# Low parts of the feed-forward input weights made by a negated copy on ScalarE and an adding DMA

## The chip, the cores and the metric

The kernel runs on one core of one Trainium2 chip. The metric is the device time of one execution in microseconds (us); the time before is the median of three runs. The core has five engines that each work through their own instructions in order: TensorE (PE in the profile, with its weight loads as PEld), VectorE (DVE), ScalarE (ACT), GpSimd (POOL) and SyncE (SP, which here only issues DMAs). Engines wait for each other, and for DMAs, by semaphores.

## The reference

The reference is a trunk of two layers on 512 tokens of width 1024 in float32: a gated linear attention (GLA) mixer with its feed-forward part, then a gated DeltaNet (GDN) mixer with its feed-forward part, each followed by a residual and a LayerNorm. What the change touches is the feed-forward part, which both layers have:

```python
def conv_ffn(x, w_in, conv_w, w_out):
    h = causal_dwconv(x @ w_in, conv_w)          # w_in: 1024 x 5632, conv_w: 3 x 5632
    gate, up = jnp.split(h, 2, axis=-1)          # 2816 columns each
    return (jax.nn.gelu(gate, approximate=False) * up) @ w_out
```

## The kernel before

Every large product is done in three matmuls on a reduced float32 format (float32r): each operand is split into a high part, its value rounded to float32r, and a low part, the difference. The products high x high, high x low and low x high are summed in PSUM. For a weight tile the split is two instructions in `split_out` (line 698): ScalarE copies the raw tile to `wh` with rounding (CAST), and VectorE subtracts it from the raw tile into `wl` (TENSOR_TENSOR).

The feed-forward input product runs over items. One item is 128 columns of `w_in`: the raw weights (128 partitions x 1024 float32, 512 KB) are loaded by a DMA on SP's queue (line 304), split, and used in 24 matmuls of 128x512 (8 blocks of the contraction, three products each, the third of which reads `wl`). Items alternate between a gate block and an up block. After an item ScalarE scales the PSUM bank by the last tap of the convolution (line 991), VectorE adds the two other taps (line 993), and for a gate block ScalarE applies Gelu (line 1011); an up block is multiplied by its gate.

The 44 items of one layer come in three groups of 16, 16 and 12. After each of the first two groups the matching rows of the output weights are multiplied in the folded form (`folded`, PSUM tiles `fold`, 14 weight items of 12 matmuls): sums of quarters of `w_out`, with tiles `b` and `raw` loaded by line 390. The last group is followed by the plain product with the last rows of `w_out` (`out_rows`, PSUM tiles `tm`): its weights are six more `raw` loads (line 321), and each half is split into a slot of its own (in the profile these slots are called `fh`, `fl` or `b`, because they are cut from tiles that the group before has left). The first rows of `tm` need the activations of all six row blocks of the last group, the last item's too.

Buffers set how far ahead this runs. There are three `raw` tiles, shared by the input weights, the `raw` quarters of the fold and the output weights, and four pairs of `wh` and `wl`. A new load into a raw tile waits until its last reader is done; a split waits until the item four before has been used. SP issues loads in one order, and a load that waits holds those behind it. The program is written as one sequence (`prefetch` issues an item's load and split two items ahead, three in the fold, five near the end of the last group), and a scheduler then sets each engine's order from its estimates; only PE's order is mostly pinned.

GpSimd does the affine step of the residual at the start of each feed-forward part (lines 903 and 904) and issues a few DMAs.

Of the kernel before, what the change touches and what calls it, by code (L numbers as in the profile page):

```python
# [8 lines left out]
F32 = mybir.dt.float32  # L9
# [4 lines left out]
ALU = mybir.AluOpType  # L14

P = 128
D = 1024
S = 512
NTB = S // P
NC = D // P  # L20
DFF = 2816
# [46 lines left out]
def blk(i, n=P):  # L68
    return slice(i * n, i * n + n)


class Trunk:
# [214 lines left out]
    def issue(self, item):  # L287

        nc = self.nc
        if item[0] == "rep":  # L290
            return self.issue_rep(*item[1:])
        if item[0] == "pad":
            return self.issue_pad(*item[1:])
        if item[0] == "fold":
            return self.issue_fold(*item[1:])
        if item[0] == "gated":
            return self.issue_gated(*item[1:])
        raw = self.rp.tile([P, 1024], F32, name=self.uid("raw"), tag="raw")
        used = 1024
        if item[0] == "fm":  # L300
            _, w, col = item
            r3 = raw.rearrange("p (c f) -> p c f", c=NC)
            w3 = w[:, col:col + P].rearrange("(c p) f -> p c f", p=P)
            part = lambda queue, c, n: queue.dma_start(r3[:, c:c + n, :], w3[:, c:c + n, :])
            if self.issued > 1:
                part(nc.sync, 0, NC)
            else:
                if self.issued == 0:
                    part(nc.scalar, 0, 4)
                    self.arriving(0, 1)  # L310
                else:
                    part(nc.sync, 0, 4)
                    self.arriving(1, 1)
                self.late.append(lambda: part(nc.sync, 4, 4))
                if self.issued:
                    for load in self.late:
                        load()
        else:
            _, w, row, n, col, _ = item
            used = n * S  # L320
            self.load = nc.sync.dma_start(
                raw[:, :used].rearrange("p (j f) -> p j f", j=n),
                w[row:row + n * P, col:col + S].rearrange("(j p) f -> p j f", p=P))
        if self.in_slots(item):
            w = []
            for j in range(used // S):
                wh, wl = self.room("wsh"), self.room("wsl")
                self.slotted = self.split_out(wh, wl, raw[:, blk(j, S)])
                self.vec(0.7)
                w.append((wh, wl))  # L330
            return w
        self.held += 1
        wh = self.wp.tile([P, 1024], F32R, name=self.uid("wh"), tag="wh")
        wl = self.wp.tile([P, 1024], F32R, name=self.uid("wl"), tag="wl")
        pieces = [blk(j, S) for j in range(used // S)] if self.issued < 2 else [slice(0, used)]
        split = lambda cols: self.split_out(wh[:, cols], wl[:, cols], raw[:, cols])
        if self.issued < 2:
            self.pieces += [lambda cols=cols: split(cols) for cols in pieces]
        elif self.issued < 4:
            self.opening(*split(pieces[0]))  # L340
        else:
            self.split = parts = split(pieces[0])
            for ins, other in zip(parts, self.after):
                if other is not None:
                    self.behind(ins, other)
        self.vec(1.24)
        return [(wh[:, blk(j, S)], wl[:, blk(j, S)]) for j in range(used // S)]
# [348 lines left out]

    def split_out(self, dst_h, dst_l, src):
        return self.nc.scalar.copy(dst_h, src), self.nc.vector.tensor_sub(dst_l, src, dst_h)  # L698

    def opening(self, *parts):  # L700

        if self.first is not None:
            for ins, other in zip(parts, self.first):
                self.behind(ins, other)
        self.first = parts
# [1321 lines left out]
```

## Time and profile before

| what | value |
| --- | --- |
| median of three runs | 1227.69 us (1227.67 to 1228.21) |
| profiled execution, span from first to last instruction | 1226.6 us (the page has no other time of this execution) |
| PE busy | 1219.4 us, 99% of the span |
| DVE busy | 928.2 us, 76% |
| ACT busy | 604.0 us, 49% |
| POOL busy | 115.1 us, 9% |
| DMA, mean over the span | 109 GB/s |
| feed-forward input product and folds, first layer | 222 to 535 us |
| the same, second layer | 873 to 1186 us |
| granted TensorE clock | 1.000 |

Times in the trace are counted from the first instruction. A row of the timeline reads: start, duration, engine, line, operation, output tile <- input tiles, shape, count, and in brackets the idle time of the engine just before with what ended it. Rows of DMA issues read: output <- input, issuing queue, count, size of one, and median time from issue to landing.

### The profile page before, as it was taken

Reading aid. Unit: us, or ns where it says so; the run is one execution under the profiler, and the core shown is the slowest. Engines: PE = TensorE matmul, PEld = TensorE weight load, DVE = VectorE, ACT = ScalarE, POOL = GpSimd, SP = SyncE. Lnnn points to the kernel's source line nnn. Section 1 sums busy time; section 2 is a strip of 40 time slices with the busy share of each in tenths; the row PEclk is TensorE's granted clock in tenths of the full one; section 3 lists DMA queues with packets and bytes.
Section 4 is the critical chain, followed back from the end, with each engine's and each line's share of the span. In section 5 each row is a group of like instructions: output and inputs, shape, how many; then the busy total and the mean of one; then the engine's idle time right before and its main releaser. Section 6 shows DMA issues by size and latency. Waiting matters only on the chain.

```text
span 1226.6 us, 17147 instructions
## 1 busy us (share of the span) xinstructions
PE 1219.4 (99%) x6530; PEld 1029.4 (84%) x6530; DVE 928.2 (76%) x1539; ACT 604.0 (49%) x1066; POOL 115.1 (9%) x159
## 2 busy tenths in 40 slices
PE   9999999999999999999999999999999999999998
PEld 8888888988888888888888888988988888888886
DVE  4966996688957895667779975688687966796667
ACT  5654764544434443554678555644644434443440
POOL 4000000700000000001152030200520000000000
PEclk9999999999999999999999999999999999999999
DMA  7432253542443123333344351245442263223321
GB/s 205 117 107 69 87 179 102 167 120 69 136 139 102 53 68 114 111 105 104 104 129 129 99 139 37 77 130 155 123 135 69 82 192 87 89 82 103 106 66 69
DMA packets 171186, 133.67 MB, mean 109 GB/s; under 512 B 16390, under 2 KB 140362, under 8 KB 171104
## 3 DMA queue, kind: packets, MB, share of 16 engines
q1 hardware_dynamic: 166272, 123.62, 34.2%
q0 software_dynamic: 3872, 8.30, 2.1%
q8 instruction: 51, 0.84, 0.3%
q10 hardware_dynamic: 960, 0.66, 0.2%
q14 instruction: 31, 0.25, 0.1%
HBM read 126.77 MB, written 5.78 MB: 108 GB/s over the span
## 4 chain that ended last, share of the span: by engine, by line
PE 98%; DMA 1%; SPq 0%; DVE 0%; ACT 0%; issue 0%; DVEq 0%
PE fm L208 54%; PE tm L208 20%; PE fold L208 16%; PE o L208 2%; PE xT L226 1%; DMA raw<-in_gla_w_in_dram 1%; PE pq L208 1%; PE pg L208 1%; PE vn L208 1%; PE yT L226 1%; PE V L208 0%; PE qs L208 0%; PE s L208 0%; PE ks L208 0%; PE ds L208 0%; PE sa L208 0%
## 5 line engine op out<-in xcount | busy, mean ns | idle before, releaser
L208 PE MATMUL fm<-xh,wh 128*128 128x512 f32 (+2 forms) x1096 | 400.4, 368 | 0.7 <-ACT xh L698 0.7
L208 PE MATMUL fm<-xl,wh 128*128 128x512 f32 (+2 forms) x1096 | 398.5, 366 | 0.0
L208 PE MATMUL fm<-xh,wl 128*128 128x512 f32 (+1 forms) x1072 | 391.5, 367 | 0.4 <-DVE wl L698 0.4
L698 DVE TENSOR_TENSOR wl<-raw,wh 128x1024 fp32r<-128x1024 f32 (+1 forms) x162 | 200.6, 1241 | 160.5 <-ACT wh L698 160.3
L698 ACT CAST wh<-raw 128x1024 fp32r<-128x1024 f32 (+1 forms) x163 | 168.9, 1038 | 221.6 <-PE fm L208 145.1
L208 PEld LDWEIGHTS fm<-xh,wh 128*128 128x128 f32 (+1 forms) x1096 | 205.4, 188 | 34.1 <-ACT xh L698 0.9
L208 PEld LDWEIGHTS fm<-xl,wh 128*128 128x128 f32 (+1 forms) x1096 | 205.4, 188 | 33.0
L208 PEld LDWEIGHTS fm<-xh,wl 128*128 128x128 f32 x1072 | 201.2, 189 | 33.8 <-DVE wl L698 0.6
L993 DVE SCALAR_TENSOR_TENSOR conv<-fm,ffn_cw,conv 128x511 f32<-128x511 f32 x112 | 83.5, 746 | 9.4 <-ACT conv L991 8.0
L208 PE MATMUL fold<-wh,fh 128*128 128x512 f32 x224 | 87.6, 391 | 0.0
L208 PE MATMUL fold<-wh,fl 128*128 128x512 f32 x224 | 87.2, 389 | 0.0
L208 PE MATMUL fold<-wl,fh 128*128 128x512 f32 x224 | 87.2, 389 | 0.0
L698 ACT CAST wh<-b 128x1024 fp32r<-128x1024 f32 x48 | 49.8, 1053 | 74.6 <-PE fold L208 31.1
L1011 ACT ACTIVATE conv<-conv 128x512 f32<-128x512 f32 x44 | 27.8, 632 | 69.0 <-DVE conv L993 69.0
L698 DVE TENSOR_TENSOR wl<-b,wh 128x1024 fp32r<-128x1024 f32 x48 | 58.0, 1223 | 4.7 <-ACT wh L698 4.7
L1543 DVE SCALAR_TENSOR_TENSOR conv<-fm,gdn_cw,conv 128x511 f32<-128x511 f32 (+2 forms) x72 | 54.1, 790 | 5.1 <-ACT conv L1541 4.5
L208 PE MATMUL tm<-wh,xh 128*128 128x512 f32 x128 | 52.6, 411 | 0.0
L208 PEld LDWEIGHTS fold<-wh,fh 128*128 128x128 f32 x224 | 42.0, 188 | 9.8 <-DVE h L1082 1.2
L208 PE MATMUL tm<-wl,xh 128*128 128x512 f32 x128 | 50.1, 391 | 0.0
L208 PE MATMUL tm<-wh,xl 128*128 128x512 f32 x128 | 50.0, 391 | 0.0
L208 PEld LDWEIGHTS fold<-wh,fl 128*128 128x128 f32 x224 | 42.0, 188 | 8.8
L208 PEld LDWEIGHTS fold<-wl,fh 128*128 128x128 f32 x224 | 42.1, 188 | 8.6
(359 smaller groups left out, 1932.5 us busy)
## 6 DMA issues: line engine op xcount, KB each, us to landing
raw<-in_ffn_w_in_dram SPq DMA_DIRECT2D x88, 512.0 KB, 3.9
raw<-in_gdn_w_in_dram SPq DMA_DIRECT2D x32, 512.0 KB, 4.1
raw<-in_ffn_w_out_dram SPq DMA_DIRECT2D x28, 512.0 KB, 3.7
raw<-in_gla_w_in_dram SPq DMA_DIRECT2D x26, 512.0 KB, 3.7
b<-in_ffn_w_out_dram SPq DMA_DIRECT2D x24, 512.0 KB, 5.5
raw<-in_gla_w_out_dram SPq DMA_DIRECT2D x8, 512.0 KB, 3.8
raw<-in_gdn_w_out_dram SPq DMA_DIRECT2D x8, 512.0 KB, 3.8
h<-in_x_dram SPq DMA_DIRECT2D x8, 256.0 KB, 4.7
```

Source lines behind the costliest of these rows:

```text
L208: t = self.nc.tensor.matmul(out, a, b, start=start, stop=stop, skip_group_check=joined)
L226: t = self.nc.tensor.transpose(out, a, self.ident[:n, :n])
L698: return self.nc.scalar.copy(dst_h, src), self.nc.vector.tensor_sub(dst_l, src, dst_h)
L993: nc.vector.scalar_tensor_tensor(a[:, d:], ps[:, :S - d], tap(2 - d), a[:, d:], ALU.mult, ALU.add)
L1011: nc.scalar.activation(a, a, AF.Gelu)
L1543: self.conv = nc.vector.scalar_tensor_tensor(a[:, d:], ps[:, :S - d], tap(3 - d), a[:, d:], ALU.mult, ALU.add)
```

## The change

For the input weights of the feed-forward parts, except those of the first four gate and first four up blocks, the low part is no longer made by VectorE. ScalarE makes the high part as before, then writes its negative into the low tile, and a DMA issued by GpSimd adds the raw tile onto it in place (raw - high). 36 of the 44 items of each layer take the new way, 72 in all.

```diff
         split = lambda cols: self.split_out(wh[:, cols], wl[:, cols], raw[:, cols])
+        if item[0] == "fm" and item[1].shape[1] == 2 * DFF and item[2] % DFF >= 4 * P:
+            self.split_dma(wh, wl, raw)
+            return [(wh[:, blk(j, S)], wl[:, blk(j, S)]) for j in range(2)]
         if self.issued < 2:
...
     def split_out(self, dst_h, dst_l, src):
         return self.nc.scalar.copy(dst_h, src), self.nc.vector.tensor_sub(dst_l, src, dst_h)
+
+    def split_dma(self, dst_h, dst_l, src):
+        self.nc.scalar.copy(dst_h, src)
+        self.nc.scalar.mul(dst_l, dst_h, -1.0)
+        self.nc.gpsimd.dma_start(dst_l.bitcast(F32), src, accum_op=ALU.add)
```

In the rows of the changed program below, lines are those of the changed file: L704 is the cast, L705 the negated copy, L706 the DMA, L701 the old split (698 before), and from there on eight lines more than before (L999 is 991, L1019 is 1011).

ScalarE at the end of the last group of the first layer, before. `wh_4382` and `wh_4388` are the last two input items of the layer; `fh_4078<-raw_4392` and the next are the first output weights.

```order
L698 CAST wh_4382<-raw_4380 128x1024
L991 ACTIVATE conv_4337<-fm_4312,ffn_cw_29_155 128x512
L698 CAST fh_4078<-raw_4392 128x512
L698 CAST fl_4079<-raw_4392 128x512
L1011 ACTIVATE conv_4337<-conv_4337 128x512
L698 CAST wh_4388<-raw_4386 128x1024
L991 ACTIVATE conv_4373<-fm_4348,ffn_cw_29_155 128x512
```

The same place in the changed program (`raw_4428` is the first raw tile of output weights).

```order
L704 CAST wh_4416<-raw_4414 128x1024
L999 ACTIVATE conv_4370<-fm_4345,ffn_cw_29_155 128x512
L705 ACTIVATE wl_4417<-wh_4416 128x1024
L1019 ACTIVATE conv_4370<-conv_4370 128x512
L701 CAST fh_4105<-raw_4428 128x512
L701 CAST fl_4106<-raw_4428 128x512
L704 CAST wh_4423<-raw_4421 128x1024
L999 ACTIVATE conv_4407<-fm_4382,ffn_cw_29_155 128x512
L705 ACTIVATE wl_4424<-wh_4423 128x1024
```

The negated copies stand behind the convolution's scaling of another item, and the casts of the output weights have moved behind the Gelu; the last input item and its scaling still stand behind them.

ScalarE at the change from the first fold to the second group, before: the last casts of the fold and the first of the group.

```order
L698 CAST wh_3983<-b_613_3685 128x1024
L698 CAST wh_4002<-b_614_3687 128x1024
L698 CAST wh_4020<-raw_4018 128x1024
L698 CAST wh_4040<-raw_4038 128x1024
L698 CAST wh_4058<-raw_4056 128x1024
```

And in the changed program:

```order
L701 CAST wh_4007<-b_613_3709 128x1024
L701 CAST wh_4026<-b_614_3711 128x1024
L704 CAST wh_4044<-raw_4042 128x1024
L705 ACTIVATE wl_4045<-wh_4044 128x1024
L704 CAST wh_4065<-raw_4063 128x1024
L705 ACTIVATE wl_4066<-wh_4065 128x1024
```

Here each negated copy follows its cast directly.

GpSimd in the changed program at the start of the first feed-forward part: the last of the residual's steps, and the first adding DMAs, which stand behind them.

```order
L911 TENSOR_TENSOR h_105<-h_105,gb_2290 128x512
L911 TENSOR_TENSOR h_106<-h_106,gb_2292 128x512
L912 TENSOR_TENSOR h_105<-h_105,gb_2294 128x512
L912 TENSOR_TENSOR h_106<-h_106,gb_2296 128x512
L706 DMA wl_2532<-raw_2529 128x1024
L706 DMA wl_2571<-raw_2568 128x1024
```

Before, nothing of a feed-forward part followed those steps on GpSimd. The loads on SP keep their order in both programs; what a load into a raw tile waits for is now the landing of the adding DMA that last read the tile, where it was VectorE's subtraction.

## The prediction

> **What bounds the kernel now.** I read the page first, then what PE waits for, then the feed-forward stretches by engine.
>
> ```profile
> span 1226.6 us, 17147 instructions
> ...
> PE 1219.4 (99%) x6530; PEld 1029.4 (84%) x6530; DVE 928.2 (76%) x1539; ACT 604.0 (49%) x1066; POOL 115.1 (9%) x159
> ```
>
> ```profile
> PE warm L772 <- POOL one L97: 1.0, 1, 1.0
> PE fm L208 <- ACT xh L698: 0.7, 1, 0.7
> PE xT L226 <- DMA h<-in_x_dram: 0.6, 1, 0.6
> PE mid L208 <- ACT diag L919: 0.6, 1, 0.6
> PE fm L208 <- DVE wl L698: 0.4, 1, 0.4
> ```
>
> These are all the waits of PE that the trace names: 3.3 us of the 7.2 in which it is not busy (1226.6 - 1219.4), at the start and the end of the program. Busy PE need not be PE at its peak, so the spacing has to be looked at too:
>
> ```profile
> 349.78 0.39 PE L208 MATMUL fm<-xh,wh 128*128 128x512 f32 x1
> 350.00 0.39 PE L208 MATMUL fm<-xl,wh 128*128 128x512 f32 x1
> 350.23 0.39 PE L208 MATMUL fm<-xh,wl 128*128 128x512 f32 x1
> ```
>
> A matmul starts every 0.2267 us, so an item of 24 takes 5.44 us, and ScalarE's casts, which wait for PE, keep just that distance (502.24 and 507.68 in the rows of ACT below). PE sets the pace, VectorE follows.
>
> ```profile
> 222.00:306.00 84.00, 84.00 (x447) 72.81 (x445) 66.28 (x79) 40.07 (x55) 18.22 (x12) 1.00 0.41 126
> 345.00:431.00 86.00, 86.00 (x381) 71.23 (x380) 61.79 (x76) 35.49 (x43) 0.00 (x0) 1.00 0.31 91
> ```
>
> In these two input groups (columns: length, then busy PE, PEld, DVE, ACT, POOL, clock, DMA share, GB/s) PE is busy throughout, DVE 72 to 79%, the DMA engines 31 to 41%. There is nothing for a relieved VectorE to give back; the question is whether the new chain of low parts stays ahead of PE.
>
> **What goes and what comes.**
>
> ```profile
> L698 DVE TENSOR_TENSOR wl<-raw,wh 128x1024 fp32r<-128x1024 f32 (+1 forms) x162 | 200.6, 1241 | 160.5 <-ACT wh L698 160.3
> L698 ACT CAST wh<-raw 128x1024 fp32r<-128x1024 f32 (+1 forms) x163 | 168.9, 1038 | 221.6 <-PE fm L208 145.1
> ```
>
> 72 subtractions leave DVE: 72 x 1.24 = 89 us off an engine that PE does not wait for, worth 0. ACT gets 72 negations of the same shape as its cast, so about 1.05 each (the trace has no such row; a cast reads and writes as many elements): 76 us, some 19% of each 5.44 us item on an engine that is under half busy in both windows. Worth 0 by itself. POOL gets 72 issues of about 0.54. In the second layer its residual work ends before the first affected cast, so the adds do not queue behind it:
>
> ```profile
> 548.14 0.54 POOL L895 DMA_DIRECT2D hd<-h  x1 [0.48 <-ACT h L865]
> ...
> 893.39 3.70 POOL L904 TENSOR_TENSOR h<-h,gb 128x512 f32<-128x512 f32 x2
> ```
>
> ```profile
> 904.93 1.04 ACT L698 CAST wh<-raw 128x1024 fp32r<-128x1024 f32 x1
> ```
>
> **The price of one adding DMA.** The trace has none. The nearest rows:
>
> ```profile
> raw<-in_ffn_w_in_dram SPq DMA_DIRECT2D x88, 512.0 KB, 3.9
> b<-in_ffn_w_out_dram SPq DMA_DIRECT2D x24, 512.0 KB, 5.5
> gw<-in_gla_w_in_dram SPq DMA_DIRECT2D x2, 512.0 KB, 5.9
> dinv<-m SPq DMA_DIRECT2D x1, 512.0 KB, 3.2
> dblk<-am POOLq DMA_DIRECT2D x16, 16.0 KB, 2.1
> ```
>
> A GpSimd DMA of almost nothing lands after 2.1; 512 KB in whole rows out of SBUF after 3.2, so 1.1 is data. Low end: the add costs a plain transfer, 3.2. High end: it costs what two loads beside each other do, 5.9. I take the middle case: it has to fetch two operands of 512 KB, so 2.1 + 2 x 1.1 = **4.3 alone**. A weight load (3.9) has about 1.9 of data on the same engines, so beside one load the add lands after 4.3 + 1.9 = **6.2**.
>
> [...]
>
> **Inside a group.** A cast starts when the item four before is done, so its item starts 3 x 5.44 = 16.3 later and reads `wl` 0.45 after that. Cast 1.05, another item's scaling 0.6, negation 1.05, issue 0.1, add 6.2: 9.0. Seven us to spare. The ring of three raw tiles: load beside an add (3.9 + 2.2 = 6.1) plus those 9.0 = 15.1 of 16.3. Also covered, by 1.2 only. Worth 0. With the high end (5.9, beside a load 7.8) the ring takes 3.9 + 3.8 + 2.8 + 7.8 = 18.3 and no longer turns in time; that way lies the second rival.
>
> **After a fold** the lead is shorter.
>
> ```profile
> 336.25 1.05 ACT L698 CAST wh<-raw 128x1024 fp32r<-128x1024 f32 x1 [1.67 <-PE fold L208]
> 344.79 0.39 PE L208 MATMUL fm<-xh,wl 128*128 128x512 f32 x1
> ```
>
> Cast and negation back to back end at 338.3, the add lands at 338.4 + 4.3 = 342.7, or 344.6 beside a load; PE wants it at 344.8. Worth 0 at four places, and from 6.4 on each loses what exceeds it.
>
> **The end of a layer** is where I expect the loss. ACT before:
>
> ```profile
> 502.24 1.05 ACT L698 CAST wh<-raw 128x1024 fp32r<-128x1024 f32 x1 [0.96 <-PE fm L208]
> 503.20 0.68 ACT L991 ACTIVATE conv<-fm,ffn_cw 128x512 f32<-128x512 f32 x1
> 507.68 1.05 ACT L698 CAST wh<-raw 128x1024 fp32r<-128x1024 f32 x1 [0.30 <-PE fm L208]
> ...
> 509.22 0.61 ACT L698 CAST fh<-raw 128x512 fp32r<-128x512 f32 x1
> ...
> 512.01 0.63 ACT L1011 ACTIVATE conv<-conv 128x512 f32<-128x512 f32 x1 [1.66 <-DVE conv L993]
> ...
> 514.08 0.68 ACT L991 ACTIVATE conv<-fm,ffn_cw 128x512 f32<-128x512 f32 x1
> ...
> 520.79 0.62 ACT L698 CAST fl<-raw 128x512 fp32r<-128x512 f32 x1
> ...
> 525.07 0.68 ACT L991 ACTIVATE conv<-fm,ffn_cw 128x512 f32<-128x512 f32 x1
> ...
> 528.57 0.62 ACT L698 CAST fh<-conv 128x512 fp32r<-128x512 f32 x1 [2.31 <-DVE conv L1039]
> 529.67 0.69 ACT L991 ACTIVATE conv<-fm,ffn_cw 128x512 f32<-128x512 f32 x1 [0.48 <-PE fm L208]
> ...
> 532.02 0.63 ACT L1011 ACTIVATE conv<-conv 128x512 f32<-128x512 f32 x1 [1.66 <-DVE conv L993]
> 535.11 0.69 ACT L991 ACTIVATE conv<-fm,ffn_cw 128x512 f32<-128x512 f32 x1 [2.46 <-PE fm L208]
> ...
> 538.13 0.62 ACT L698 CAST b<-conv 128x512 fp32r<-128x512 f32 x1 [2.33 <-DVE conv L1039]
> ```
>
> ```profile
> 504.58 17.75 SPq L321 DMA_DIRECT2D raw<-in_ffn_w_out_dram  x6
> ```
>
> ```profile
> 538.80 0.74 PE L208 MATMUL tm<-fh,b 128*128 128x512 f32 x2
> ```
>
> The first output load goes out at 504.58, as soon as DVE has subtracted the item cast at 502.24. Now its raw tile is held longer: cast 502.24, scaling, negation until 504.8, add issued at 504.9, landed at 511.1 (6.2, a load runs beside it). The load then runs beside the next add, issued at 510.3: 3.9 plus the add's 2.2 of data less the 0.8 by which that is ahead, 5.3, so it lands at 516.4. ACT reaches the cast of that tile at 512.6, behind its Gelu, and stands until 516.4. Behind it in ACT's order are the last input item's cast and the scaling that stood at 514.08: now 516.4 + 2 x 0.52 + 0.95 = 518.4, 4.3 late. The last negation ends at 520.0; its add, beside the next output load, lands at 526.3; the load into that tile runs beside yet another output load (3.9 + 1.9) and lands at 532.2. ACT asked for it at 520.79 before and now stands in front of it, with the scaling of 525.07 three casts behind: 532.2 + 3 x 0.52 = 533.8. From there to the last item's scaling the work waits only for itself: scaling, two taps on DVE, product and cast as from 525.07 to 528.57 (3.5), that cast's own slot (0.53), scaling, taps and Gelu as from 529.67 to 532.02 (2.35), and the Gelu's slot (0.53): 533.8 + 6.9 = 540.7 instead of 535.11. That is 5.6 late, and PE has no slack: its matmul at 538.80 follows the last activation's cast of 538.13 at once. **PE stands about 5.6 us at each of two layer ends**, which have the same orders: 11.2.
>
> **Sum:** 1226.6 + 11.2 = 1237.8 for the profiled execution; the median of the runs lies 1.1 above its span, so 1238.9, say **1239**.
>
> **Rivals.** First, *the add is quick and all is hidden.* At 3.2 it lands at 508.2, the first output load at 512.1, before ACT asks at 512.6; the last add is then out of the way by 520, and one late load is caught up, since the scalings wait for PE every 5.44. Time 1227 to 1230. For it: 1.1 of data is small. Against: it must touch two operands.
>
> Second, *the DMA engines become the bound.* Their share in the groups is 0.31 to 0.41, 1.9 of each 5.44 us. If an add holds all engines for 4.4 instead of 2.2, an item needs 6.3: 0.86 more for 72 items is 62, and each layer end loses roughly twice as much, 22 in all: near 1310. It decides from (5.44 - 1.9) = 3.5 us of data per add. For it: `b` loads at 5.5 show engines already shared. Against: the dinv row.
>
> Third, *faster*: DVE's 89 us let something start earlier. It would have to come out of the 7.2 us in which PE is not busy, none of it in the two groups shown; bounded by 1220. That the low parts do not take the new way is excluded by the instructions counted in the changed program (72 fewer on DVE, 72 more on ACT and POOL).
>
> [...]
>
> **How the numbers follow.** Layer ends stand still (1233 to 1250): 0.50. Hidden: 0.17. Bound by DMA engines or on the way there (1250 up): 0.29. Faster: 0.04. A measurement of this kernel tells 0.2%, 2.5 us, from no change: faster 0.04, same 0.17, slower 0.79. The range runs from the hidden case's 1228 to 1285, which takes in most of the way to the DMA bound and leaves out its far end (about 0.13) and little below.
>
> **What would show it.** Adds landing in 4 to 6.5 us; a PE wait of 4 to 7 us before the first `tm` matmuls that read the last activation, near 539 and 1190, and none inside the groups; on ACT waits of some us for `raw<-in_ffn_w_out_dram`. Wrong at the price if adds land below 3.8 (no wait) or above 8 (waits after folds and within groups); wrong in mechanism if PE waits there for other things than ScalarE's activations, or gains anywhere.

## The result, and the profile after

The changed kernel takes 1245.97 us (median of four runs, 1245.76 to 1246.38); the kernel before, timed beside it, takes 1227.93. The ratio is 1.0147, with an interval of 1.0135 to 1.016: slower by 18 us. The profiled execution grew from a span of 1226.6 to one of 1244.4, by 17.8, and its mean granted TensorE clock fell from 1.000 to 0.993.

The head of the page of the changed kernel:

```profile
span 1244.4 us, 17435 instructions
...
PE 1225.0 (98%) x6530; PEld 1032.1 (83%) x6530; DVE 845.8 (68%) x1467; ACT 673.7 (54%) x1138; POOL 177.9 (14%) x231
```

DVE lost 82 us of work and ACT gained 70, as the change intends. PE counts as many matmuls as before, but is busy for 1225.0 us instead of 1219.4: 5.6 more for the same work. The other 12.2 of the 17.8 are time in which it isn't busy. What PE waits for in the changed kernel (total, times, longest):

```profile
PE tm L208 <- ACT b L701: 9.1, 2, 4.7
PE tm L208 <- ACT fh L701: 2.6, 2, 2.3
...
PE fold L208 <- DVE wl L701: 0.5, 2, 0.3
```

Two waits at each of the two layer ends, 11.7 in all, both of the output product (`tm`) for activations that ScalarE casts (`b` and `fh` are slots here); and 0.5 in the folds. None of these was there before. 11.7 + 0.5 + 5.6 = 17.8, the whole growth (two small waits at the start are 0.6 us shorter, and the stretch after the last matmul is 0.4 longer).

PE at the end of the first layer, from the timeline of the changed kernel:

```profile
539.00 0.73 PE L208 MATMUL tm<-fl,fh 128*128 128x512 f32 x2 [2.26 <-ACT fh L701]
539.73 0.50 PE L208 MATMUL tm<-fl,fl 128*128 128x512 f32 x1
...
545.41 1.22 PE L208 MATMUL tm<-fh,b 128*128 128x512 f32 x2 [4.37 <-ACT b L701]
```

The same stretch by windows of 3 us (length, busy PE and its matmuls, clock, DMA share, GB/s):

```profile
538.00:541.00 3.00, 2.00 (x5) 0.86 0.79 209
541.00:544.00 3.00, 0.04 (x1) 0.50 0.00 0
544.00:547.00 3.00, 1.59 (x4) 0.50 0.00 0
547.00:550.00 3.00, 3.00 (x9) 0.50 0.00 0
550.00:553.00 3.00, 3.00 (x14) 0.94 0.66 175
```

Here is most of the 5.6 us of extra busy time. The clock falls to 0.50 about 1.2 us after the first stall and stays there until some five microseconds after the second: in the window from 547 PE never waits, and yet does 9 matmuls where an undisturbed window holds 14 or 15. At the end of the second layer it stands 0.37 and 4.72 us, and windows at a clock of 0.50 follow again. At this clock PE is busy for 5.9 us at the first layer end and 3.7 at the second; half of that, 4.8 us, is put down to the clock, an estimate from the granted 0.50 (the matmuls from 547.29 to 549.85 start 0.43 us apart instead of 0.2267). The other 0.8 is not the clock: the first matmuls behind a stall start about 0.36 us apart instead of 0.2267, at a granted clock that is still 1.00 (two in 0.73 us from 539.00).

What led to the stall stands on ScalarE's timeline and on SP's:

```profile
504.62 1.05 ACT L704 CAST wh<-raw 128x1024 fp32r<-128x1024 f32 x1 [2.33 <-DMA raw<-in_ffn_w_in_dram]
...
509.12 1.05 ACT L704 CAST wh<-raw 128x1024 fp32r<-128x1024 f32 x1
...
518.46 0.62 ACT L701 CAST fh<-raw 128x512 fp32r<-128x512 f32 x1 [5.41 <-DMA raw<-in_ffn_w_out_dram]
...
532.99 0.62 ACT L701 CAST fl<-raw 128x512 fp32r<-128x512 f32 x1 [3.38 <-DMA raw<-in_ffn_w_out_dram]
...
541.75 0.67 ACT L999 ACTIVATE conv<-fm,ffn_cw 128x512 f32<-128x512 f32 x1
...
544.74 0.62 ACT L701 CAST b<-conv 128x512 fp32r<-128x512 f32 x1 [2.33 <-DVE conv L1047]
```

```profile
514.10 15.47 SPq L321 DMA_DIRECT2D raw<-in_ffn_w_out_dram  x6
```

The output loads, which went out from 504.58 on before, start at 514.10. ScalarE stands 5.41 and 3.38 us for them, the last item's scaling moves from 535.11 to 541.75, and the cast that PE waits for moves from 538.13 to 544.74.

The adding DMAs by themselves, from the table of DMA issues (count, size, median us from issue to landing):

```profile
raw<-in_ffn_w_in_dram SPq DMA_DIRECT2D x88, 512.0 KB, 4.9
wl<-raw POOLq DMA_DIRECT2D x72, 512.0 KB, 5.7
```

The view of the low tiles (`wl`) gives the spread of the 72 adds:

```profile
DMA to landing us min/median/max: 4.5/5.7/8.4
```

An add lands after 5.7 us in the middle; the quickest took 4.5 and the slowest 8.4. The input loads beside them went from 3.9 to 4.9. The groups of instructions of the new chain (busy time, mean ns of one, idle time before them):

```profile
L705 ACT ACTIVATE wl<-wh 128x1024 fp32r<-128x1024 f32 x72 | 75.8, 1053 | 0.7
...
L706 POOL DMA_DIRECT2D wl<-raw x72 | 62.0, 861 | 494.8 <-ACT wl L705 229.0 <-PE fold L208 196.9 <-PE fm L208 48.7
```

And the two input groups whose windows the prediction showed (busy PE, PEld, DVE, ACT, POOL, clock, DMA share, GB/s):

```profile
222.00:306.00 84.00, 84.00 (x443) 72.64 (x442) 56.02 (x70) 47.88 (x62) 26.03 (x20) 1.00 0.67 170
345.00:431.00 86.00, 86.00 (x381) 71.23 (x380) 44.79 (x60) 48.59 (x57) 11.17 (x13) 1.00 0.82 184
```

PE doesn't stand for one moment in them, although the DMA engines are now busy for 0.67 and 0.82 of the time, from 0.41 and 0.31. In the second, where every item is new, that is (0.82 - 0.31) x 5.44 = 2.8 us more for each item.

### The profile page after: what moved, and what is told of

Its sections match the earlier page's. It is cut to its first block, busy times and chain, and to the rows that moved or that the text cites. A ratio compares the mean times of both kernels' runs of the same rounds, so it can differ in the third digit from the quotient of the medians.

```text
span 1244.4 us, 17435 instructions
## 1 busy us (share of the span) xinstructions
PE 1225.0 (98%) x6530; PEld 1032.1 (83%) x6530; DVE 845.8 (68%) x1467; ACT 673.7 (54%) x1138; POOL 177.9 (14%) x231
## 4 chain that ended last, share of the span: by engine, by line
PE 82%; DMA 8%; DVE 6%; issue 2%; ACT 2%; SPq 0%; DVEq 0%; POOLq 0%; ACTq 0%; POOL 0%
PE fm L208 43%; PE tm L208 19%; PE fold L208 11%; DMA raw<-in_ffn_w_in_dram 3%; DMA raw<-in_ffn_w_out_dram 2%; DMA wl<-raw 2%; PE o L208 2%; DVE conv L1001 1%; PE xT L226 1%; DVE wl L701 1%; DVE b L406 1%; DVE fl L701 1%; PE pq L208 1%; PE pg L208 1%; PE vn L208 1%
## 5 line engine op out<-in xcount | busy, mean ns | idle before, releaser
L701 DVE TENSOR_TENSOR wl<-raw,wh 128x1024 fp32r<-128x1024 f32 (+1 forms) x90 | 112.0, 1249 | 47.5 <-ACT wh L701 47.2
L701 ACT CAST wh<-raw 128x1024 fp32r<-128x1024 f32 (+1 forms) x91 | 92.9, 1025 | 83.7 <-PE fm L208 39.7
L706 POOL DMA_DIRECT2D wl<-raw x72 | 62.0, 861 | 494.8 <-ACT wl L705 229.0
L704 ACT CAST wh<-raw 128x1024 fp32r<-128x1024 f32 x72 | 75.4, 1048 | 96.1 <-DMA raw<-in_ffn_w_in_dram 76.3
L1001 DVE SCALAR_TENSOR_TENSOR form<-fm,ffn_cw,form 128x511 f32<-128x511 f32 x64 | 47.8, 747 | 73.0 <-ACT form L999 72.0
L705 ACT ACTIVATE wl<-wh 128x1024 fp32r<-128x1024 f32 x72 | 75.8, 1053 | 0.7
L701 ACT CAST wh<-b 128x1024 fp32r<-128x1024 f32 x48 | 49.5, 1052 | 46.9 <-PE fold L208 23.4
L911 POOL TENSOR_TENSOR h<-h,gb 128x512 f32<-128x512 f32 x16 | 24.0, 1517 | 257.2 <-PE tm L208 193.6
L701 ACT CAST fh<-form 128x1792 fp32r<-128x1792 f32 (+3 forms) x24 | 28.7, 1195 | 55.5 <-DVE form L1042 42.1
L701 DVE TENSOR_TENSOR wl<-b,wh 128x1024 fp32r<-128x1024 f32 x48 | 57.7, 1215 | 0.3 <-ACT wh L701 0.3
```

The lines of the kernel that those rows point to most:

```text
L705: self.nc.scalar.mul(dst_l, dst_h, -1.0)
L706: self.nc.gpsimd.dma_start(dst_l.bitcast(F32), src, accum_op=ALU.add)
L911: nc.gpsimd.tensor_mul(h[hf], h[hf], gb[hf])
L1001: nc.vector.scalar_tensor_tensor(a[:, d:], ps[:, :S - d], tap(2 - d), a[:, d:], ALU.mult, ALU.add)
```

## The experiments

The theory throughout: a raw tile is held until its add has landed; at a layer end this delays the output weights that are to be loaded into it; ScalarE, which works in order, stands for them with the last items' steps behind it; and PE stands for ScalarE. Rivals are ScalarE's 76 us of negations, and the adds' load on the DMA engines wherever they are. The kernel before takes 1227.8 to 1228.0 beside all these runs.

**Which group it comes from.** Two kernels do the change on a part of the items only: the first two groups (48 adds), and the last group of each layer (24 adds).

```diff
-        if ... item[2] % DFF >= 4 * P:
+        if ... 4 * P <= item[2] % DFF < 16 * P:     # first groups
+        if ... item[2] % DFF >= 16 * P:             # last group
```

> The new low parts only in the first two groups of each layer (48 of 72 adds); the last group's 24 items are split as before. Theory A (raw tiles held by the adds make the output weights late at the end of a layer, PE stands there, and its clock is halved after): no adds near a layer end, so 1227.9 within 0.2%, no PE wait before the first tm matmuls and a clock of 1.000. Rival B (the 72 negations make ScalarE late everywhere): two thirds of the loss, about 1240. Rival C (adds slow all DMAs and with them the groups): about 1240 too.

> The new low parts only in the last group of each layer (24 of 72). Theory A: the whole loss, 1245 to 1247, with PE waits of 5 to 7 us at each layer end and the clock halved after. Rivals B and C: one third of it, about 1234.

The first groups alone: 1232.23 us (1230.77 to 1236.52), ratio 1.0041 (1.0025 to 1.0057). The last group alone: 1247.68 (1246.03 to 1248.26), 1.0163 (1.0146 to 1.018). A third of the adds makes the whole loss. PE's waits with the last group's adds are those of the change:

```profile
PE tm L208 <- ACT b L701: 8.8, 2, 4.7
PE tm L208 <- ACT fh L701: 2.9, 2, 2.6
```

The other 48 adds are not quite free, though; the theory had them at nothing. Their PE wait is another one:

```profile
PE fold L208 <- DVE wl L701: 2.2, 2, 1.2
```

**ScalarE's part.** The negation stays on ScalarE, and VectorE adds the raw weight onto it; no DMA.

```diff
-        self.nc.gpsimd.dma_start(dst_l.bitcast(F32), src, accum_op=ALU.add)
+        self.nc.vector.tensor_add(dst_l, src, dst_l)
```

> All 72 items with ScalarE's cast and negation as in the change, but VectorE adds the raw tile instead of a DMA. Theory A: the raw tile is free some 2 us later than before instead of 7, so no stall: 1227.9 within 0.2%. Rival B: the whole loss stays, about 1246. Rival C: no DMA added, so 1228.

1227.70 us (1227.16 to 1228.31), ratio 0.9999 (0.999 to 1.0009), and no wait of `tm`. The negations cost nothing; that rival falls.

**Another room for the output weights.** All 72 adds stay, but the last output weights are loaded into a tile that is idle then (`form`), so that they need not wait for a raw tile.

```diff
-        raw = self.rp.tile([P, 1024], F32, name=self.uid("raw"), tag="raw")
+        if item[0] == "tm" and item[1].shape[0] == DFF:
+            raw = ...            # half of a form tile
+        else:
+            raw = self.rp.tile([P, 1024], F32, name=self.uid("raw"), tag="raw")
```

> The change as it is, but the output weights of the last group are loaded into a tile that is idle there (form) instead of the ring of three raw tiles, so that their loads no longer wait for an add. All 72 adds and negations stay. Theory A: most of the loss goes, 1228 to 1232, with PE waits of at most 2 us at a layer end and a clock near 1.000. Rival B: 1246. Rival C: the adds are all there, 1244 to 1246.

1236.69 us (1234.61 to 1237.81), ratio 1.007 (1.0055 to 1.0085). Half of the loss went, less than expected. ScalarE at the two layer ends of this kernel, then SP at the first and the second:

```profile
531.77 0.62 ACT L709 CAST b<-form 128x512 fp32r<-128x512 f32 x1 [5.55 <-DMA form<-in_ffn_w_out_dram]
...
1184.09 1.14 ACT L709 CAST b<-form 128x512 fp32r<-128x512 f32 x2 [0.57 <-DMA form<-in_ffn_w_out_dram]
```

```profile
514.97 11.17 SPq L312 DMA_DIRECT2D raw<-in_gdn_w_in_dram  x3
526.18 1.09 SPq L329 DMA_DIRECT2D form<-in_ffn_w_out_dram  x2
...
1180.30 0.88 SPq L329 DMA_DIRECT2D form<-in_ffn_w_out_dram  x2
```

At the first layer end the last two `form` loads stand on SP behind loads of the next layer's weights, which go into raw tiles and wait for adds; they go out at 526.2, ScalarE stands 5.55, and PE 2.96. The second layer has no next one; there ScalarE stands 0.57 and PE not at all. So the held tile had come back through the queue. To test this, the same kernel with these loads on GpSimd's queue:

```diff
-            self.load = nc.sync.dma_start(
+            queue = nc.gpsimd if w.shape[0] == DFF else nc.sync
+            self.load = queue.dma_start(
```

> As the run in which the last rows of the output weights are loaded into form tiles (1236.7), but these loads go out on GpSimd's queue and not on SP's. In that run ScalarE stood 5.55 us for such a load at the first layer end and 0.57 at the second; SP had issued it at 526.2, behind three loads of the next layer's weights into raw tiles that wait for adds, which the second layer end hasn't. Theory (what was left there is SP's order behind a raw tile still held): no wait before tm, clock 1.000, only waits of fold on VectorE of 2 to 3 us; span 1229 to 1230, median 1230 to 1233. Rival (the loads themselves are slow beside the adds): the stall of about 3 us at the first layer end stays, 1235 to 1238.

1230.75 us (1228.50 to 1234.84, ten runs), ratio 1.0026 (1.0016 to 1.0037); no wait of `tm` is left, and what PE stands beyond its waits of before, 3.6 us, is all in the folds. With 72 adds in place, 15 of the 18 us are gone.

**Which adds of the last group.** Only the last four items' adds in each layer (8 in all), and all but these (64).

```diff
+        if ... item[2] % DFF >= 20 * P:               # last four
+        if ... 4 * P <= item[2] % DFF < 20 * P:       # not the last four
```

> Only the last two gate and the last two up blocks of each layer take the new way: 8 adds in all. Theory (held raw tiles of the last items, standing ScalarE, stall, halved clock): nearly the whole loss of the run with the last group's 24 adds, waits of tm of 4 to 6 us at each layer end, clock 0.993 to 0.996, 1238 to 1246. Rival (a cost per add): 1227.8 + 8/24 x 19.9 = 1234.4, without a wait of more than 2 us.

> The change on all its items except the last two gate and the last two up blocks of each layer, which are split as before: 64 of the 72 adds stay. Theory (at the layer end only adds on raw tiles that the output weights are to be loaded into cost something; there are three raw tiles): no wait before tm, clock 1.000, only waits of fold on VectorE of 2 to 3 us as in the run with the first groups' adds: 1229 to 1233. Rival (each add in the last group costs its share of that run's 19.9 us, 24 adds): 1227.8 + 16/24 x 19.9 + 4.4 for the first groups = 1245.

Without the last four items' adds: 1231.40 us (1229.46 to 1234.89), ratio 1.0031 (1.0021 to 1.0042), no wait of `tm`. The last four items' adds are needed for the stall, as the theory says. But alone they make only 1236.30 (1234.36 to 1238.09), ratio 1.0068 (1.0053 to 1.0083), below what was expected. With the 16 adds before them, which alone cost nothing at the layer end, the loss is more than twice that (19.9 us in the kernel with the last group's adds, against 8.3). ScalarE's and SP's rows in the kernel with the last four only, and PE at both its layer ends:

```profile
501.42 1.05 ACT L704 CAST wh<-raw 128x1024 fp32r<-128x1024 f32 x1 [1.51 <-PE fm L208]
...
514.51 0.62 ACT L701 CAST fh<-raw 128x512 fp32r<-128x512 f32 x1 [3.73 <-DMA raw<-in_ffn_w_out_dram]
...
528.02 0.62 ACT L701 CAST fl<-raw 128x512 fp32r<-128x512 f32 x1 [2.41 <-DMA raw<-in_ffn_w_out_dram]
```

```profile
509.99 15.58 SPq L321 DMA_DIRECT2D raw<-in_ffn_w_out_dram  x6
```

```profile
540.46 0.73 PE L208 MATMUL tm<-fh,b 128*128 128x512 f32 x2 [2.35 <-ACT b L701]
...
1194.21 0.73 PE L208 MATMUL tm<-fh,b 128*128 128x512 f32 x2 [2.42 <-ACT b L701]
```

The cast at 501.42 is that of the last item but two, whose raw tile the first output load is to get. Here it waits for PE, as before (502.24). In the changed kernel the same cast stands at 504.62 and waits for its own raw tile: the ring of three tiles is already behind when the layer end comes. ScalarE's waits for input weights say the same of the whole program, first before, then in the changed kernel:

```profile
ACT wh L698 <- DMA raw<-in_ffn_w_in_dram: 7.3, 5, 2.4
```

```profile
ACT wh L704 <- DMA raw<-in_ffn_w_in_dram: 76.3, 25, 8.2
```

Where it falls behind shows in the casts after the last fold of the first layer, first before, then in the changed kernel:

```profile
461.54 1.05 ACT L698 CAST wh<-raw 128x1024 fp32r<-128x1024 f32 x1 [1.67 <-PE fold L208]
...
470.28 1.06 ACT L698 CAST wh<-raw 128x1024 fp32r<-128x1024 f32 x1 [1.67 <-PE fold L208]
```

```profile
460.66 1.05 ACT L704 CAST wh<-raw 128x1024 fp32r<-128x1024 f32 x1 [1.67 <-PE fold L208]
...
474.61 1.05 ACT L704 CAST wh<-raw 128x1024 fp32r<-128x1024 f32 x1 [6.41 <-DMA raw<-in_ffn_w_in_dram]
...
489.91 1.05 ACT L704 CAST wh<-raw 128x1024 fp32r<-128x1024 f32 x1 [3.09 <-DMA raw<-in_ffn_w_in_dram]
```

While PE is still in the fold, the first three items are cast 2.7 us apart. The fourth, the second row of each, needs the first one's raw tile again. Before, it waits for PE alone and comes 8.74 us after the first cast; in the change it waits until the add has freed the tile and the next load has filled it, and comes 13.95 us after. That is some 5 us later than in the kernel with the last four items' adds only, where it stands at 469.46. From then on the ring turns in 15.30 and 14.71 us (474.61, 489.91, 504.62), while PE takes 16.3 for three items. So it makes up ground, but not all of it: at 504.62 it is still 3.2 us behind. The fourth cast after each of the other three folds waits likewise, 4.61, 5.08 and 8.24 us.

So there are two parts: the adds of the last four items hold the tiles (2.4 us of stall at each layer end), and the adds before them bring the ring there late (the rest of the 11.7). Late alone costs little there: without the last four items' adds the same cast stands at 505.55, and PE doesn't wait; in the kernel with 48 adds, below, it stands at 505.21, and PE waits 0.9 at most.

**What the first groups' adds cost.** The kernel above without any adds on the last four items ahead of a fold either; 48 stay.

```diff
+        if ... 4 * P <= item[2] % DFF < 20 * P and item[2] % DFF // P not in (6, 7, 14, 15):
```

> The change, but the last two gate and last two up blocks ahead of each fold and ahead of the output product are split as before (48 of the 72 adds stay, inside the groups and right after the folds). Theory (what the run without the last four items' adds still lost, 1231.4 against 1228.0 with 0.2 to 0.9 us of fold waiting for VectorE, is again raw tiles held ahead of other weights, here the quarters of the folds): no wait of fold on VectorE above 0.3 us, 1227.5 to 1229.0, ratio 0.9995 to 1.001. Rival (the adds cost something wherever they stand, by their load on the DMA engines): 48/64 of the 3.4 us stay, 1230.5 or more, ratio 1.002 or more.

1229.19 us (1227.95 to 1230.26, eleven runs), ratio 1.0008 (0.9999 to 1.0017). The wait of the folds is gone. The median is 0.2 above the range of the theory and well below what the rival asked for. Of the 3.4 us that the kernel with 64 adds loses, 1.2 are left, in waits of other kinds:

```profile
PE tm L208 <- ACT b L701: 1.2, 2, 0.9
...
PE fm L208 <- DMA wl<-raw: 0.7, 1, 0.7
```

The second is the first item after a fold, at 1122.07 us: its add, issued at 1115.32, came 0.7 late. Most of the small loss too is thus tiles held ahead of other weights, not the adds as such.

**The clock.** Is it the stall that halves the clock, and not something else that goes on there? The change, with 10 matmuls into an unused PSUM bank where PE stands first at each layer end, and 20 where it stands again: 2 x 30 x 0.2267 = 13.6 us of added work.

```diff
+                        if tb == 0 and hf == 0 and c >= 4:
+                            pad = self.psum("pad")
+                            for _ in range(FILL[c - 4]):          # FILL = (10, 20)
+                                filler = self.mm(pad, self.xh[:, 0, :P], self.xh[:, 0, :])
```

> The change, and at each layer end 30 more matmuls (high part of the layer's input by itself, 128x512) into a PSUM bank that nobody reads: 10 ahead of the first group of tm matmuls that stands, 20 ahead of the second. At 0.2267 us each they are 2.27 and 4.53 us of work on data that is long there, put where PE stood 2.26 + 4.37 and 0.37 + 4.72 us. Theory (the stall itself halves TensorE's clock, and that is the 5.6 us of busy time that the change added): with PE kept at work the granted clock stays 1.000, the waits before tm go, and the time is before's span plus the filling plus some 0.5 of waits at the folds, 1226.6 + 2 x 6.8 + 0.5 = 1240.7, about 1242.3 for the median (1241 to 1244), though 13.6 us of work were added. Rival (the clock falls for another reason, such as the transfers or the engines at work there): clock again 0.993, the lost 5.6 us stay, 1244.4 + (13.6 - 11.7) = 1246.3, about 1248 for the median, or more.

Its profiled execution: the head of the page, and the windows at the first layer end.

```profile
span 1242.2 us, 17555 instructions
...
PE 1233.9 (99%) x6590; PEld 1041.1 (84%) x6590; DVE 846.7 (68%) x1467; ACT 674.6 (54%) x1138; POOL 177.5 (14%) x231
```

```profile
539.00:542.00 3.00, 2.74 (x11) 1.00 0.63 171
542.00:545.00 3.00, 3.00 (x15) 1.00 0.00 0
545.00:548.00 3.00, 2.37 (x10) 1.00 0.00 0
```

The clock stays at 1.00, with the same transfers and the same work of the other engines around it. PE is busy 1233.9 - 13.6 = 1220.3 us for the kernel's own work, 4.7 less than in the change; that is the 4.8 put down to the clock above, and 0.9 more than before remain. With 13.6 us of work added this execution is 2.2 shorter in span. But the median of the runs, 1248.09 (1243.91 to 1250.97), isn't: it is where the rival had it, though the clock was 1.000 in every one of these executions, which the rival excluded. Two more runs were to say where the longer executions lose: twice the filling, and the same kernel once more.

> As the filled run (clock 1.000 in its executions, but 1243.9 to 1251.0), with 20 and 40 matmuls instead of 10 and 20 at each layer end, 13.6 us where PE stood some 6. Theory (the filling of 6.8 us was not long enough in the executions that took longer, and what stood over was short enough to leave the clock alone): 1226.6 + 27.2 + 0.5 = 1254.3 of span, about 1256 for the median, all executions within 2 us, clock 1.000. Rival (the longer executions lost elsewhere, in the groups or at the folds): median 1258 to 1263 and a spread of some 7 us as before, clock 1.000.

> The filled kernel once more, for one profile: its executions took 1243.9, 1246.8, 1249.4 and 1251.0, and the profile was of the quickest. Theory: what an execution takes beyond 1242.3 is found as waits of PE before tm at the layer ends (0.9 us in the first profile). Rival: it is found as waits in the groups or at the folds (0.2 there).

With twice the filling, 27.2 us: 1257.56 (1256.02 to 1259.23), all at a clock of 0.999 or 1.000; no wait of `tm` is left, 1.6 us in the folds, and one of 1.0 outside the feed-forward parts. The median lies between theory and rival. The spread went from 7 us to 3, and 13.6 us of further work made the median 9.5 longer, which suggests, with four executions each, that part of the spread lay at the layer ends. The second profile of the first filling (1245.27) shows 0.6 us of waits of `tm` and 1.5 in the folds, against 0.9 and 0.2 in the first (1243.91): most of the 1.4 us between these two lies in the folds, as the rival had it. The two longest executions, 1249.4 and 1251.0, were not profiled, and where they lost their time stays open. That the clock's fall hangs on PE's standing is shown; that the time lost to it comes back in every run when PE is kept busy is not.

## Why the prediction was right or wrong

**The time** was right to 7 us: 1239 forecast, 1246.0 measured, slower, through PE standing at both layer ends for an activation that ScalarE delivers late. Waits of 11.2 us were forecast there, and 11.7 measured.

**The step that failed** is the sum itself: "1226.6 + 11.2" counts a stall at its own length. These stalls cost more, since TensorE then works at a granted clock of 0.50 for a while, 10.2 us at the first layer end and 6.8 at the second: 4.8 us of the 17.8 in the profile, and most of the gap of 7 between 1239 and 1246. The rest of the gap is 0.8 us of slower matmuls right behind the stalls, 1.0 of longer waits, and 0.5 by which the median lies further above the profiled span than before. The prediction looked at clocks only to read them as 1.00. At the first layer end the mean of 0.86 from 538 to 541 puts the fall at about 540.2, after one stall of 2.26 us, when PE was at work again; the matmuls resumed at 545.4 behind the second stall, and the clock was back at 550.4, 5.0 us later. At the second they resumed at 1205.5, and the window from 1209 to 1212 has a mean clock of 0.97, so it was back at about 1209.2, 3.7 us later. The last section has a stall of 2.42 us that the clock fell after and one of 2.35 that it didn't fall after.

**The layer end** came out right by two errors that cancel, which is luck. The working took the casts of the last items at the times that they had before, that is, a layer end that meets an undisturbed ring. The kernel with the last four items' adds is that case, and it shows 2.4 us of stall, not 5.6. The first output load was forecast to land at 516.4 and landed by 514.5; the tile that the second wait of ScalarE is for was forecast at 532.2 and was there at 528.0. Some 0.8 of each is the program's being that much earlier there (the cast at 501.42 instead of 502.24). What was too dear is mostly the load that "runs beside yet another output load": it was put at 3.9 + 1.9 = 5.8, and in that kernel it goes out at 524.18 and lands at 528.00, 3.8 later. Some 1.4 more lie in the first add and the first output load, which took 5.6 and 4.5 where 6.2 and 5.3 were forecast.

The second error made up for it: the cast on which the first output load hangs came at 504.62 where 502.24 was reckoned with, because the ring reached the layer end late. **Inside a group** it had been put at 15.1 of 16.3, "Worth 0", and in the last group that was nearly right: it turned in 15.30 and 14.71, and PE doesn't stand there. What the prediction missed is the ring **after a fold**, where it looked only at whether the first item's low part is there in time. The fourth item's raw tile is not: three casts come 2.7 us apart, then one turn of the ring has to pass, and a cover of 1.2 us a turn doesn't make up the 5 us in the rest of a group. Not all of ScalarE's 76.3 us of waiting comes from there. In the first group, which no fold precedes, the cast at 270.33 is 3.2 us late too; why, no run separates.

**The price of the add** was nearly right: 4.3 alone and 6.2 beside a load were forecast, 4.5 is the least and 5.7 the median. The prediction's estimate, 2.1 us of a DMA of almost nothing and twice the 1.1 us of data of a plain transfer, comes near the least: 4.3 against 4.5, where the plain transfer of this size (`dinv<-m`) took 3.2. The runs show the add's time; that it pays for two operands, they don't. GpSimd's issue was too cheap at 0.54; it takes 0.86.

**For PE after a fold** 0 was forecast, with 0.2 us to spare and a loss from a price of 6.4 on. The change has no PE wait there; the kernel with 48 adds has one, of 0.67, where an add took some 6.7. **Ahead of a fold** the prediction didn't look. There too other weights are loaded into raw tiles, and the adds held them: 0.5 us in the change, 2.2 in the kernel with the first groups alone.

**The moved work** was rightly put at nothing: 82 us less on VectorE gained nothing, and 76 us of negations cost nothing (0.9999 with the negations alone).

**The rivals.** That the add is quick and hidden fell with its price. That the DMA engines become the bound was nearer than its condition made it look: it was to decide at 3.5 us of data per add, and 2.8 more per item were measured. What it forecast, PE waits within the groups, didn't come. The faster case had no support in any run.

## What to carry to other kernels

When an operand's tile is released later, follow the tile and not the engine that was relieved: the cost shows where the ring hands over to another kind of load, on an engine that works in order, or in a queue behind a load that waits. Price such a step with the ring's state as the change leaves it, not with the times of the profile before. Check the ring also where several tiles are taken in quick succession, as here after a fold, and ask how many turns it needs to make up what it loses there. And add to a stall of TensorE the time at half clock that may follow it: here some 4.8 us on top of 11.7.

## What the runs showed of the hardware that was not expected

Stalls of nearly the same length did or did not halve the clock. In the kernel with the last four items' adds PE stood 2.35 us at the first layer end and 2.42 at the second. Its windows at both:

```profile
539.00:542.00 3.00, 1.54 (x7) 1.00 0.00 0
542.00:545.00 3.00, 3.00 (x15) 1.00 0.06 10
```

```profile
1193.00:1196.00 3.00, 1.79 (x7) 0.90 0.00 0
1196.00:1199.00 3.00, 3.00 (x9) 0.53 0.00 0
```

After the first the clock stayed at 1.00. After the second it fell 1.2 us after PE had resumed at 1194.2, and PE did 9 matmuls in the 3 us from 1196 instead of 15. The mean clocks of windows of 0.5 and 1 us put its changes at 540.2, 550.4, 1202.3 and 1209.2 in the changed kernel, at 1195.4 and 1198.8 here, and at 542.4 and 545.8 in the kernel with another room, where PE stood 2.96 us. So the stretches at 0.50 last 10.2, 6.8, 3.4 and 3.4 us. The two long ones are those of the changed kernel: the first holds the whole stall of 4.37 us, the second 3.1 us of the one of 4.72. The two short ones go with single stalls of 2.42 and 2.96.

A stall of some 2.3 us can be enough, then, and can also pass: the clock fell after 2.26 us in the changed kernel and after 2.42 here, and stayed at 1.00 after 2.35. So the length of the stall alone doesn't decide in these three; what does, no run here shows.

A second point is the price of an adding DMA. 512 KB onto a tile in SBUF take 4.5 to 8.4 us from issue to landing, and GpSimd needs 0.86 us to issue it, against 0.54 for the plain transfer of 256 KB (`hd<-h`) in the prediction's rows.
